# A hybrid decoder layer on one core: 192 columns of first weights instead of 256, the rotary tables behind the first norm, the attention norm by halves, the first keys and values among the input tiles

## The chip, the core and the metric

One core of a Trainium2 chip runs the whole layer as one program. TensorE (PE) does the matrix products and reads its operands from SBUF, the on-chip memory; its sums arise in PSUM. VectorE (DVE), ScalarE (ACT) and GpSimd (POOL) do the elementwise work, and the queue of SyncE (SP) issues the DMAs between HBM and SBUF. Every engine works off its own instruction list in order, and they wait for one another by semaphores. The metric is the device time of one execution in microseconds (us), the median over runs; lower is better.

## The reference

The layer has sequence length 1024, width 1024, 8 attention heads and float32 throughout. Shortened:

```
u = rmsnorm(h, g_mix);  z = u @ w_in          # x_rnn 512 | x_gate 512 | c_q 256 | c_kv 128 | k_rope 32
y_rnn = rglru_group(x_rnn, x_gate, ...)       # conv over 4 steps, two gates, linear recurrence, gelu(x_gate)
q  = rmsnorm(c_q) @ w_q_up                    # per head 64 nope + 32 rotary columns
kv = rmsnorm(c_kv) @ w_kv_up                  # per head 64 key + 64 value columns
q_rope, k_rope = apply_rope(...)              # cos and sin of position * frequency
y_att = causal softmax attention (8 heads, query blocks of 128)
h = h + concat(rmsnorm(y_rnn), rmsnorm(y_att)) @ w_out
h = h + (silu(rmsnorm(h) @ w_ffn_gate) * (rmsnorm(h) @ w_ffn_up)) @ w_ffn_down    # inner width 2816
h = h + sigmoid(rmsnorm(h) @ w_ple_gate) * rmsnorm(p @ w_ple_proj)
return rmsnorm(h, g_final)
```

## The kernel before

**Products.** Activations are kept transposed: features on the 128 partitions, the 1024 positions along the row. Each float32 operand is split into a high part and a low part of a shorter format, and each product is three matmuls, high by high, high by low and low by high (`x_h`, `x_l` and `w_h`, `w_l` in the trace). The usual matmul is 128x512: one 128x128 weight block against half of the positions.

**Order.** The code doesn't emit instructions as it goes. It records them in a `Plan`; `Plan.order` then runs a list scheduler with modelled costs over all engines, and on each engine takes the ready operation with the smallest key. The key is the number of the operation in the recording, plus `plan.shift` at that moment, plus a few fixed offsets (line 232). PSUM is given out in two pools, four banks of 512 columns and two wide buffers of 1024, and SBUF in 51 slots of one size; an operation can only start when its tile has a place. All instructions are emitted by one line (372), so every row of the trace has L372, and only names of tiles tell them apart.

**Stages, in the trace's time.**
- 0 to 39 us: the input `x` arrives in eight blocks k of 128 features (`xr`) and is split into `x_h` (ACT) and `x_l` (DVE); its squares are added up in `x_acc` (DVE). For each k the weights `w1[k]`, 256 columns wide, give two tiles `g`: `g1[0]` holds the 128 columns of c_kv, `g1[1]` the rotary key columns, k and its swapped halves, each laid out twice (32+32+32+32). Each block is 12 matmuls: 2 tiles, 2 halves of the positions, 3 products. In between stand the first products of c_q (`wn_a`, `wn_b`). `nx_ms` sums `x_acc` over the partitions, `nx_bc` spreads the reciprocal root over them, `nx_rb` is the copy of it with which every later tile is scaled (`ckv`, `krz`, `cq`, `zr`, `zg`).
- The generator `tables()` works out the angles (`ang`, `turns`), sine and cosine (`sc`, `cse`), and the constants of the recurrence (`q`, `cpos`).
- 50 to 165 us: eight input tiles in the order of `IN_ORDER` (`in_tile`, r0 to r3 recurrent, g0 to g3 gate), with the recurrence between (`rg_*`). Behind the last but one come the rotary keys (`make_rope_keys`), the keys of the first heads (`make_k`, tiles `kps`, `k_h`, `k_l`), queries (`make_q`, `qps`) and values (`make_v`, `v`).
- 165 to 350 us: attention head by head (`s` scores, `pA` and `pB` exponentials, `tp` transposes, `av`), with the first half of the output product (`wo<-yr`) in between. `ya` is the attention's result, four tiles of 1024 positions; `y_acc` the sum of its squares.
- 338 to 428 us: the attention norm (`na_ms`, `na_bc`, `na_rb`), the scaled and split `ya_h` and `ya_l`, and the output product `wo`.
- 428 to 1057 us: the feed-forward layer. Its gate and up products use weights `wg`, `wu`; the inner activations `hx` go to HBM and come back for the down product, which runs over c = 0 to 3 (inner blocks) and j (output blocks), j = 0 to 15 in all. Each j needs a pair of weight tiles `wd_r`, which `pump("d", j)` loads and splits; each c needs its `hx` tiles, seven groups, worked off one after the other at the first j of the c.
- 1057 us to the end: the gated embedding (`plg`, `ple`) and the last norm.

Of the kernel before, what the change touches and what calls it, by code (L numbers as in the profile page):

```python
# [8 lines left out]
F32R = mybir.dt.float32r  # L9
BF16 = mybir.dt.bfloat16  # L10
I32 = mybir.dt.int32
AF = mybir.ActivationFunctionType
ALU = mybir.AluOpType
# [3 lines left out]
P = 128  # L17
S = 1024
# [25 lines left out]
IN_ORDER = "r0 r1 r2 r3 g0 g1 g2 g3".split()  # L44
# [334 lines left out]
XLATE = 40  # L379
HOLD = 0.15  # L380
KLATE = 100
HL = 5
HAT = 3
NWIDE = 2
# [8 lines left out]
def hybrid_layer(ctx, tc, xT, pT, pos, vec, const, const2, w1, wn, wrg, wq, wkv, wo, wg, wu, *rest):  # L393
    plan = Plan(tc.nc)
# [9 lines left out]
    def slot(name, dt=F32):  # L404
        return plan.tile(big, [P, S], dt, name, "slot", NSLOT)
# [29 lines left out]
    def f(ap):  # L435
        return ap.bitcast(F32)
# [19 lines left out]
    def load_w(src, name, cols=S):  # L456
        raw = wslot(name + "_raw")
        Y.dma_start(out=raw[:, :cols], in_=src)
        hi = wslot(name + "_h", F32R)
        lo = wslot(name + "_l", F32R)  # L460
        A.activation(hi[:, :cols], raw[:, :cols], AF.Copy)
        V.tensor_sub(lo[:, :cols], raw[:, :cols], f(hi)[:, :cols])
        return hi, lo

    Q = [slice(0, HB), slice(HB, S)]
# [34 lines left out]
            yield  # L500


    order = [(("w1", k), w1[k], 256) for k in range(8)] + [(("wn", i), wn[i], S) for i in range(2)]
    order += [(("rg", 0), wrg, S)] + [(("wn", i), wn[i], S) for i in range(2, 10)]
    order += [(("wkv", 0), wkv, S), (("wq", 0), wq[0], S)]
    order += [(("wq", 1), wq[1], S)]
# [20 lines left out]
    def col(name, i=0):  # L527
        c = VEC[name] + i
        return vc[:, c:c + 1]
# [65 lines left out]
    def tables():  # L595

        pi = slot("pos_i", I32)
        Y.dma_start(out=pi, in_=pos.to_broadcast([P, S]))
        ang = slot("ang")
        V.tensor_copy(ang, pi)  # L600
        V.tensor_scalar_mul(ang, ang, INVF)
        kk = slot("turns")
        V.tensor_scalar(kk, ang, 0.15915494309189535, 12582912.0, op0=ALU.mult, op1=ALU.add)
        V.tensor_scalar_add(kk, kk, -12582912.0)
        for cpart in (6.0, 0.28125, 0.0019353071795864769):
            V.scalar_tensor_tensor(out=ang, in0=kk, scalar=-cpart, in1=ang, op0=ALU.mult, op1=ALU.add)
        V.scalar_tensor_tensor(out=kk, in0=ang, scalar=-1.0, in1=ang, op0=ALU.mult, op1=ALU.max)
        V.tensor_scalar(kk, kk, BETA, GAMMA, op0=ALU.mult, op1=ALU.add)
        V.scalar_tensor_tensor(out=ang, in0=ang, scalar=ALPHA, in1=kk, op0=ALU.mult, op1=ALU.add)
        sc = slot("sc")  # L610
        yield
        A.activation(sc, ang, AF.Sin)
        cse = slot("cse")
        G.memset(cse[0:64], ATT_SCALE)
        A.activation(cse[64:128], sc[64:128], AF.Copy, scale=ATT_SCALE)


        plan.hold = plan.ops[-1]
        lL = vc[:, VEC["lru_L"]:VEC["lru_L"] + 4]
        nl, al, e4, s4, z4, po = [small([P, 4], f"q4_{i}", bufs=1) for i in range(6)]  # L620
        V.tensor_scalar_mul(nl, lL, -1.0)
        V.tensor_max(al, lL, nl)
        A.activation(e4, al, AF.Exp, scale=-1.0)
        V.tensor_scalar_add(s4, e4, 2.0)
        V.reciprocal(s4, s4)
        V.tensor_mul(s4, s4, e4)
        V.tensor_mul(z4, s4, s4)
        V.memset(po, 1.0 / 19.0)
        for d in (17, 15, 13, 11, 9, 7, 5, 3, 1):
            V.tensor_mul(po, po, z4)  # L630
            V.tensor_scalar_add(po, po, 1.0 / d)
        V.tensor_mul(po, po, s4)
        V.tensor_scalar_max(nl, nl, 0.0)
        V.scalar_tensor_tensor(out=po, in0=po, scalar=2.0, in1=nl, op0=ALU.mult, op1=ALU.add)
        cpos = small([P, 4], "cpos", bufs=1)
        cneg = small([P, 4], "cneg", bufs=1)
        V.tensor_scalar_mul(cpos, po, LRU_C)
        V.tensor_scalar_mul(cneg, po, -LRU_C)
        plan.hold = None
        tabs.extend((sc, cse, cpos, cneg))  # L640


# [3 lines left out]
    for k in range(8):  # L646
        xr = slot("xr")
        if k == 0:
            if X0 == 1:
                Y.dma_start(out=vc, in_=vec)  # L650
            if X0 == 2:
                Y.dma_start(out=xr[:, HS[0]], in_=xT[k][:, HS[0]])
                Y.dma_start(out=vc, in_=vec)
            wh, wl = weight(("w1", k), 0)
            x2 = (slot("x_h", F32R), slot("x_l", F32R))
            for h in range(2):
                if not (X0 == 2 and h == 0):
                    Y.dma_start(out=xr[:, HS[h]], in_=xT[k][:, HS[h]])
                A.activation(x2[0][:, HS[h]], xr[:, HS[h]], AF.Copy, scale=col("g_mix", 0))
                V.scalar_tensor_tensor(out=x2[1][:, HS[h]], in0=xr[:, HS[h]], scalar=col("g_mix", 0),  # L660
                                       in1=f(x2[0])[:, HS[h]], op0=ALU.mult, op1=ALU.subtract)
        else:
            Y.dma_start(out=xr, in_=xT[k])
            wh, wl = weight(("w1", k))
            x2 = split(xr, col("g_mix", k), "x")
        if k == 1:
            Y.dma_start(out=cs, in_=const)
        if k == TK:
            tb = tables()
            next(tb)  # L670
        xs.append(x2)

        plan.shift = XLATE
        sq_acc(acc, xr, k == 0, V)
        plan.shift = 0
        for i in range(2):
            c = slice(i * P, (i + 1) * P)
            mm(g1[i][:2], wh[:, c], wl[:, c], x2, k == 0, k == 7)

    if TK == 8:  # L680
        tb = tables()
# [157 lines left out]
    tasks.append(cq_task())  # L839
    step()  # L840
    rgw = weight(("rg", 0), 1)
    for it in IN_ORDER[:-1]:
        if it == "g2":
            weight(("wkv", 0), 0)
            weight(("wq", 0), 0)
        in_tile(it)


    wqr = {}
    qs, ks, vt = {}, {}, []  # L850
# [129 lines left out]
    ys = []  # L980
# [20 lines left out]
    def two():  # L1001
        return both("wo", len(ops) % 3 < 2)

    kvh, kvl = weight(("wkv", 0), 1)
    wqr[0] = weight(("wq", 0), 1)
    make_rope_keys()
    make_k(0)
    make_q(0, 0)
    in_tile(IN_ORDER[-1])
    for b in range(3):  # L1010
        make_v(b)
    step()
    for qb in range(4):
        scores(0, qb)
        make_v(3 + qb)
    make_q(0, 1)
    make_v(7)

# [76 lines left out]
    res = []  # L1095
    hs, xf, hd = {}, {}, {}
    facc = slot("f_acc")
    for _ in rstd_steps(yacc[0], 512, "na", res):
        pass
    for j in range(4):  # L1100
        V.tensor_mul(ya[j], ya[j], res[0])
        ys.append(split(ya[j], col("g_att", j), "ya"))

    def make_x(va, vb, name):

# [159 lines left out]
    def down(c, m, xs, mid, after=None):  # L1265
        j = 4 * c + m

        def ahead(i):
            pump("d", j)
            if i >= 3:  # L1270
                pump("d", j + 1)
            mid(i)
            if c == 0 and i == HAT and m < 3:
                reload_h(m + 1)
# [166 lines left out]
def _layout(a):  # L1441
# [14 lines left out]
    k[:, C_ID:C_ID + P] = np.eye(P)  # L1456
    i = np.arange(P)
    k2 = np.zeros((P, 2 * P), np.float32)
    k2[:, :P] = (i[:, None] < 64) & (i[:, None] % 32 == i[None] % 32)
    k2[:, P:] = np.where(i[None] > i[:, None], NEG, 0.0)  # L1460
    o["const2"] = k2
    r = i % 64
# [8 lines left out]
    ckv = np.r_[1280:1408]  # L1471
    kr = np.r_[1408:1440]
    ksw = np.r_[1424:1440, 1408:1424]
    o["w1"] = c(w3[:, :, np.concatenate([ckv, kr, ksw, kr, ksw])])

    def ntile(w, cols):
        return w[:, cols].reshape(-1, P, len(cols)).transpose(1, 0, 2).reshape(P, -1)
# [56 lines left out]
```

## Time and profile before

| What | Value |
|---|---|
| Median of 3 runs | 1192.4 us (1192.07 to 1193.71) |
| The profiled execution | 1192.32 us, of which the trace's span is 1190.5 us |
| Mean granted TensorE clock | 0.995 of full speed |
| PE busy | 1161.9 us, 98% of the span |
| DVE, ACT, POOL busy | 983.7, 646.4, 234.9 us |

The span reaches from the first to the last instruction; 1.8 us of the execution lie around it. "Busy" counts a matmul until its modelled end, and matmuls overlap, so PE can be busy and slow at once.

### The profile page before, as it was taken

How to read it: one execution, taken by the hardware profiler on the slowest of the kernel's cores; microseconds unless marked ns; L12 is line 12 of the kernel's file. 1: busy time of each engine (PE TensorE's matmuls, PEld its weight loads, DVE VectorE, ACT ScalarE, POOL GpSimd, SP SyncE). 2: the span in 40 equal slices, each digit the busy share in tenths (PEclk: the TensorE clock that was granted, in tenths of full speed). 3: DMA queues.
4: the chain of work that ended last, by engine and by line, in shares of the span. 5: the costliest groups of instructions: out<-in, count | busy, mean ns of one | idle time of the engine just before them, and what ended most of it. 6: DMA issues, size and time to landing. Idle time of an engine off the chain costs nothing.

```text
span 1190.5 us, 15414 instructions
## 1 busy us (share of the span) xinstructions
PE 1161.9 (98%) x5608; PEld 964.9 (81%) x5608; DVE 983.7 (83%) x1482; ACT 646.4 (54%) x1085; POOL 234.9 (20%) x133
## 2 busy tenths in 40 slices
PE   8999999999999999999999999999999999999996
PEld 6788878888878878888888888888887887887896
DVE  7978788888978599889888888878997758785987
ACT  8447977877846265454444544444332214376565
POOL 0001240312102132333123321333000000244000
PEclk9999999999999999999999999999999999999998
DMA  9001100000305123344423544266968764032342
GB/s 343 19 18 36 36 1 1 2 1 1 134 26 195 72 107 124 124 177 184 170 102 129 195 160 157 106 250 223 358 243 280 261 243 160 36 124 89 108 175 72
DMA packets 47676, 155.91 MB, mean 131 GB/s; under 512 B 5360, under 2 KB 8688, under 8 KB 47600
## 3 DMA queue, kind: packets, MB, share of 16 engines
q1 hardware_dynamic: 47600, 154.93, 35.5%
q8 instruction: 44, 0.72, 0.2%
q14 instruction: 32, 0.26, 0.1%
HBM read 109.82 MB, written 45.09 MB: 130 GB/s over the span
## 4 chain that ended last, share of the span: by engine, by line
PE 83%; DVE 9%; ACT 4%; DMA 2%; issue 2%; SPq 0%; DVEq 0%; ACTq 0%
PE ff_z L372 29%; PE ff_y L372 14%; PE ff_x L372 7%; PE wo L372 5%; PE plg L372 4%; PE s L372 4%; PE wn L372 4%; PE av L372 2%; PE tp L372 2%; PE qps L372 1%; PE wn_b L372 1%; PE wn_a L372 1%; DVE h L372 1%; DMA wd_r<-in_wd 1%; PE wo_a L372 1%
## 5 line engine op out<-in xcount | busy, mean ns | idle before, releaser
L372 POOL TENSOR_TENSOR silu<-silu,nf_rb 128x512 f32<-128x512 f32 x77 | 123.8, 1632 | 278.1 <-DVE silu L372 257.8
L372 PE MATMUL ff_z<-hx,wd 128*128 128x512 f32 x528 | 128.6, 390 | 2.9 <-ACT wd L372 1.7
L372 PE MATMUL ff_z<-x,wg 128*128 128x512 f32 x528 | 128.0, 390 | 0.2 <-DVE x L372 0.2
L372 PE MATMUL ff_z<-x,wu 128*128 128x512 f32 x528 | 127.1, 389 | 0.0
L372 PEld LDWEIGHTS ff_z<-hx,wd 128*128 128x128 f32 x528 | 98.5, 188 | 25.1 <-ACT wd L372 2.1
L372 PEld LDWEIGHTS ff_z<-x,wg 128*128 128x128 f32 x528 | 98.9, 188 | 21.8 <-DVE x L372 0.9
L372 PEld LDWEIGHTS ff_z<-x,wu 128*128 128x128 f32 x528 | 99.0, 188 | 20.7 <-ACT ff_u L372 0.2
L372 ACT ACTIVATE hx<-silu 128x512 fp32r<-128x512 f32 x55 | 34.6, 629 | 71.3 <-DVE silu L372 42.1
L372 PE MATMUL ff_y<-hx,wd 128*128 128x512 f32 x264 | 65.3, 389 | 0.0
L372 PE MATMUL ff_y<-x,wg 128*128 128x512 f32 x264 | 64.3, 390 | 0.7 <-ACT x L372 0.7
L372 PE MATMUL ff_y<-x,wu 128*128 128x512 f32 x264 | 63.6, 389 | 0.0
L372 ACT ACTIVATE wd<-wd_r 128x256 fp32r<-128x256 f32 (+2 forms) x64 | 29.9, 491 | 60.2 <-DMA wd_r<-in_wd 21.4
L372 PE MATMUL plg<-hg_h,wpg_h 128*128 128x256 f32 (+1 forms) x192 | 61.7, 321 | 0.6 <-ACT wpg_h L372 0.3
L372 PE MATMUL plg<-hg_l,wpg_h 128*128 128x256 f32 (+1 forms) x192 | 61.1, 318 | 0.0
L372 PE MATMUL plg<-hg_h,wpg_l 128*128 128x256 f32 (+1 forms) x192 | 61.0, 319 | 0.0
L372 DVE TENSOR_TENSOR h<-ff_z,h 128x512 f32<-128x512 f32 x64 | 43.8, 686 | 20.6 <-PE ff_z L372 20.2
L372 POOL TENSOR_TENSOR p_acc<-p_acc,sq 128x1024 f32<-128x1024 f32 x7 | 18.2, 2595 | 214.0 <-ACT sq L372 214.0
L372 PEld LDWEIGHTS ff_y<-x,wg 128*128 128x128 f32 x264 | 49.4, 188 | 11.5 <-ACT x L372 1.1
L372 PEld LDWEIGHTS ff_y<-hx,wd 128*128 128x128 f32 x264 | 49.6, 188 | 10.4
L372 PEld LDWEIGHTS ff_y<-x,wu 128*128 128x128 f32 x264 | 49.6, 188 | 10.3
L372 ACT ACTIVATE wd<-wd_s 128x256 fp32r<-128x256 f32 (+2 forms) x48 | 23.5, 498 | 63.3 <-DVE wd_s L372 48.1
L372 ACT ACTIVATE silu<-silu 128x512 f32<-128x512 f32 x44 | 27.8, 632 | 53.4 <-POOL silu L372 52.9
(407 smaller groups left out, 3048.2 us busy)
## 6 DMA issues: line engine op xcount, KB each, us to landing
hx<-hx SPq DMA_DIRECT2D x140, 512.0 KB, 3.8
wg_r<-in_wg SPq DMA_DIRECT2D x22, 512.0 KB, 5.1
wu_r<-in_wu SPq DMA_DIRECT2D x22, 512.0 KB, 3.4
wpg_raw<-in_wpg SPq DMA_DIRECT2D x20, 512.0 KB, 3.5
wn_raw<-in_wn SPq DMA_DIRECT2D x10, 512.0 KB, 7.2
wo_raw<-in_wo SPq DMA_DIRECT2D x8, 512.0 KB, 4.5
h<-in_xT SPq DMA_DIRECT2D x8, 512.0 KB, 4.4
hd<-h SPq DMA_DIRECT2D x8, 512.0 KB, 3.2
```

The costliest lines, as they stand in the source:

```text
L372: getattr(self.engines[o.eng], o.fn)(*a, **k)
```

## The change

Five things, each in its own place of the code:

1. `load_w` makes the low part only for the first 128 columns of a 192-column weight tile in a tile of its own; the low part of the 64 columns left over is written beside their high part, into columns 192 to 255 of the `hi` tile. The weights `w1` come with 192 columns (c_kv, the rotary columns once). So one 128-column block holds 64 high and 64 low columns of the rotary keys, and `g1[1]` takes four matmuls for each k (x_h and x_l, two halves) instead of six; high and low land in different rows of the result, which the constant matrix `const2` then adds together.
2. In `tables()` a shift of 300 is put on the angle tables and on the recurrence's constants.
3. The attention norm, with its scaling and splitting, has a shift of -200, and the first of the four `ya` tiles is scaled and split by halves of the positions.
4. `make_rope_keys` is called at tile g1, `make_k(0)` at g2, and four of the eight `make_v` ahead of the last input tile.
5. In the down product `pump("d", j + 1)` is called from step i = 1 of a j and no longer from i = 3.

```diff
+NV0 = 4
+TL = 300
+NAE = -200
...
-        V.tensor_sub(lo[:, :cols], raw[:, :cols], f(hi)[:, :cols])
+        full = cols - cols % P
+        V.tensor_sub(lo[:, :full], raw[:, :full], f(hi)[:, :full])
+        if full < cols:
+            V.tensor_sub(hi[:, cols:full + P], raw[:, full:cols], f(hi)[:, full:cols])
...
-    order = [(("w1", k), w1[k], 256) for k in range(8)] + [(("wn", i), wn[i], S) for i in range(2)]
+    order = [(("w1", k), w1[k], 192) for k in range(8)] + [(("wn", i), wn[i], S) for i in range(2)]
...
+        plan.shift = TL
         V.tensor_copy(ang, pi)
...
+        mm(g1[0][:2], wh[:, :P], wl[:, :P], x2, k == 0, k == 7)
         for i in range(2):
-            c = slice(i * P, (i + 1) * P)
-            mm(g1[i][:2], wh[:, c], wl[:, c], x2, k == 0, k == 7)
+            for h in range(2):
+                T.matmul(g1[1][h], lhsT=wh[:, P:2 * P], rhs=x2[i][:, HS[h]], start=k == 0 and i == 0, stop=k == 7 and i == 1)
...
-    kvh, kvl = weight(("wkv", 0), 1)
+    for it in IN_ORDER[:-1]:
+        if it == "g1":
+            kvh, kvl = weight(("wkv", 0), 0)
+            make_rope_keys()
+        if it == "g2":
+            weight(("wq", 0), 0)
+            make_k(0)
+        in_tile(it)
+    for b in range(NV0):
+        make_v(b)
     wqr[0] = weight(("wq", 0), 1)
-    make_rope_keys()
-    make_k(0)
     make_q(0, 0)
     in_tile(IN_ORDER[-1])
-    for b in range(3):
-        make_v(b)
     step()
     for qb in range(4):
         scores(0, qb)
-        make_v(3 + qb)
+        if NV0 <= 3 + qb:
+            make_v(3 + qb)
...
+    plan.shift = NAE
     for _ in rstd_steps(yacc[0], 512, "na", res):
         pass
     for j in range(4):
-        V.tensor_mul(ya[j], ya[j], res[0])
-        ys.append(split(ya[j], col("g_att", j), "ya"))
+        hi, lo = slot("ya_h", F32R), slot("ya_l", F32R)
+        for c in HS if j == 0 else [slice(0, S)]:
+            V.tensor_mul(ya[j][:, c], ya[j][:, c], res[0][:, c])
+            A.activation(hi[:, c], ya[j][:, c], AF.Copy, scale=col("g_att", j))
+            V.scalar_tensor_tensor(out=lo[:, c], in0=ya[j][:, c], scalar=col("g_att", j), in1=f(hi)[:, c],
+                                   op0=ALU.mult, op1=ALU.subtract)
+        ys.append((hi, lo))
+    plan.shift = 0
...
             pump("d", j)
-            if i >= 3:
+            if i >= 1:
                 pump("d", j + 1)
...
-    k2[:, :P] = (i[:, None] < 64) & (i[:, None] % 32 == i[None] % 32)
+    k2[:, :P] = i[:, None] % 32 == i[None] % 32
...
-    o["w1"] = c(w3[:, :, np.concatenate([ckv, kr, ksw, kr, ksw])])
+    o["w1"] = c(w3[:, :, np.concatenate([ckv, kr, ksw])])
```

**The first place is DVE between the last blocks of `x` and the first norm.** Before, the angle table's instructions stand between the sums of squares:

```order
L372 SCALAR_TENSOR_TENSOR x_l<-xr,vc,x_h 128x1024
L372 SCALAR_TENSOR_TENSOR ang<-turns,ang 128x1024
L372 TENSOR_TENSOR x_acc<-x_acc,sq 128x1024
L372 SCALAR_TENSOR_TENSOR ang<-turns,ang 128x1024
L372 TENSOR_TENSOR rg_l<-rg_raw,rg_h 128x1024
L372 SCALAR_TENSOR_TENSOR turns<-ang 128x1024
L372 TENSOR_TENSOR x_acc<-x_acc,sq 128x1024
L372 TENSOR_SCALAR turns<-turns,cs 128x1024
L372 TENSOR_TENSOR x_acc<-x_acc,sq 128x1024
L372 SCALAR_TENSOR_TENSOR ang<-ang,cs,turns 128x1024
```

Now the first of them stand behind the norm's last small operation (`n_r`), and ahead of the scaling of the first tiles:

```order
L372 TENSOR_TENSOR n_r<-n_r_403,n_t 128x8
L372 CAST ang<-pos_i 128x1024
L372 TENSOR_SCALAR ang<-ang,cs 128x1024
L372 TENSOR_SCALAR turns<-ang 128x1024
L372 TENSOR_TENSOR cq_438<-wn_a,nx_rb 128x512
L372 TENSOR_TENSOR ckv<-g_93,nx_rb 128x1024
L372 TENSOR_TENSOR krz<-g_100,nx_rb 128x1024
L372 TENSOR_TENSOR cq_438<-wn_b,nx_rb 128x512
L372 TENSOR_SCALAR turns<-turns 128x1024
L372 TENSOR_TENSOR wn_l<-wn_raw,wn_h 128x1024
L372 SCALAR_TENSOR_TENSOR ang<-turns,ang 128x1024 x3
```

All ten instructions on `ang` and `turns` have left the stretch ahead of `n_ss`, and three of them now precede the scaling that empties the PSUM tiles `g`.

**The second place is PE at the attention norm.** Names ending in `_h` and `_l` are high and low parts; what stands in brackets are the engines that a matmul waits for. Before, the first product of the new operand takes whole tiles:

```order
L372 MATMUL na_bc<-cs,n_r 128x128 [waits PE_49]
L372 MATMUL na_bc<-cs,n_r 128x128 x3
L372 MATMUL wo_b<-yr_l,wo_h 128x512
L372 MATMUL wo_a<-yr_h,wo_l 128x512
L372 MATMUL wo_b<-yr_h,wo_l 128x512
L372 MATMUL wo<-ya_h,wo_h 128x512 [waits Activation_49]
L372 MATMUL wo<-ya_h,wo_h 128x512 x3
L372 MATMUL wo_a<-ya_h,wo_h 128x512
L372 MATMUL wo_b<-ya_h,wo_h 128x512
L372 MATMUL wo<-ya_l,wo_h 128x512 [waits DVE_49]
```

Now:

```order
L372 MATMUL na_bc<-cs,n_r 128x128 x3
L372 MATMUL wo_a<-yr_h,wo_l 128x512
L372 MATMUL wo_b<-yr_h,wo_l 128x512
L372 MATMUL wo_a<-yr_h,wo_h 128x512
L372 MATMUL wo_b<-yr_h,wo_h 128x512
L372 MATMUL wo_a<-yr_l,wo_h 128x512
L372 MATMUL wo_b<-yr_l,wo_h 128x512
L372 MATMUL wo_a<-yr_h,wo_l 128x512
L372 MATMUL wo_b<-yr_h,wo_l 128x512
L372 MATMUL wo<-ya_h,wo_h 128x512 [waits Activation_49]
L372 MATMUL wo<-ya_h,wo_h 128x512
L372 MATMUL wo_a<-ya_h,wo_h 128x512
```

Eight old products now stand behind `na_bc` where there were three, and the wait for the second half of `ya_h` comes three matmuls later.

**The third place is SP's queue in the down product**, around the weights of j = 12, the first j of c = 3. Before:

```order
L372 DMA hx<-hx_5_6247 128x1024
L372 DMA hx<-hx_5_6553 128x1024
L372 DMA hx<-hx_5_6859 128x1024
L372 DMA wd_r_8567<-in_wd 128x1024
L372 DMA wd_r_8577<-in_wd 128x1024
L372 DMA hx<-hx_5_7208 128x1024
```

Now:

```order
L372 DMA hx<-hx_4_7166 128x1024
L372 DMA wd_r_8541<-in_wd 128x1024
L372 DMA wd_r_8551<-in_wd 128x1024
L372 DMA hx<-hx_5_6242 128x1024
L372 DMA hx<-hx_5_6548 128x1024
L372 DMA hx<-hx_5_6854 128x1024
L372 DMA hx<-hx_5_7203 128x1024
```

The pair of `wd_r` has moved ahead of three tiles of the sixth `hx` group; at j = 8 it has moved ahead of two in the same way.

## Rows read from the trace of the kernel before

**Rows 1.** What PE waited for over the whole span: total, times, longest.
```profile
PE wo L372 <- ACT ya_h L372: 2.5, 1, 2.5
PE ff_z L372 <- ACT wd L372: 1.7, 1, 1.7
PE v L372 <- DVE v L372: 1.6, 1, 1.6
PE s L372 <- ACT pB L372: 1.4, 2, 1.2
PE ff_z L372 <- DVE h L372: 1.2, 1, 1.2
PE wn_a L372 <- DVE wn_l L372: 0.6, 1, 0.6
```

**Rows 2.** The chain that ended last: start us, us, what, in the down product.
```profile
973.32 9.31 DMA wd_r<-in_wd
...
1016.41 2.72 PE ff_x L372 x12
```

**Rows 3.** Timeline of PE in the first stage: start us, us, operation, tiles, count.
```profile
14.29 0.73 PE L372 MATMUL g<-x_l,w_h 128*128 128x512 f32 x2
...
39.24 0.99 PE L372 MATMUL nx_ms<-cs,x_acc 128*128 128x128 f32 x7
```

**Rows 4.** Timeline of DVE in the first stage.
```profile
12.96 1.28 DVE L372 SCALAR_TENSOR_TENSOR x_l<-xr,vc,x_h 128x1024 fp32r<-128x1024 f32 x1
...
37.96 1.22 DVE L372 TENSOR_TENSOR x_acc<-x_acc,sq 128x1024 f32<-128x1024 f32 x1
```

**Rows 5.** Windows, instructions on the tile ang alone: window, length, DVE busy (count), ACT busy, clock.
```profile
20.00:41.00 21.00, 8.29 (x8) 0.59 (x1) 1.00 0.44 177
```

**Rows 6.** Timeline of ACT at the end of the first norm.
```profile
48.34 0.60 ACT L372 ACTIVATE nx_rb<-nx_bc 128x512 f32<-128x512 f32 x1 [0.52 <-PE nx_bc L372]
```

**Rows 7.** Timeline of DVE before the attention.
```profile
114.42 2.28 DVE L372 TENSOR_TENSOR_SCAN rg_h<-rg_r,rg_i 128x1024 f32<-128x1024 f32 x1
...
148.12 3.90 DVE L372 TENSOR_TENSOR_SCAN rg_h<-rg_r,rg_i 128x1024 f32<-128x1024 f32 x1
152.03 3.73 DVE L372 TENSOR_TENSOR k_l<-kr,k_h 64x512 fp32r<-64x512 f32 x6
...
164.41 4.26 DVE L372 TENSOR_TENSOR v<-v 128x256 fp32r<-128x256 f32 x12
```

**Rows 8.** Timeline of POOL in the same stretch.
```profile
147.02 2.85 POOL L372 TENSOR_TENSOR r_acc<-r_acc,sq 128x1024 f32<-128x1024 f32 x1 [13.52 <-ACT sq L372]
```

**Rows 9.** Windows of the input tiles: PE, PEld, DVE, ACT, POOL busy (counts), clock, DMA share, GB/s.
```profile
50.00:160.00 110.00, 110.00 (x503) 91.33 (x502) 92.31 (x112) 73.40 (x83) 16.44 (x6) 1.00 0.07 25
```

**Rows 10.** Timeline of ACT at the first scores.
```profile
174.79 0.69 ACT L372 ACTIVATE pA<-s,nm 128x512 f32<-128x512 f32 x1 [0.29 <-DVE nm L372]
```

**Rows 11.** Timeline at the attention norm, of PE, ACT and DVE.
```profile
346.25 1.03 PE L372 MATMUL na_bc<-cs,n_r 128*128 128x128 f32 x8
...
346.94 1.09 ACT L372 ACTIVATE na_rb<-na_bc 128x512 f32<-128x512 f32 x2 [3.48 <-PE na_bc L372]
...
348.06 3.50 DVE L372 TENSOR_TENSOR ya<-ya,na_rb 128x1024 f32<-128x1024 f32 x3 [3.55 <-ACT na_rb L372]
...
349.32 3.48 ACT L372 ACTIVATE ya_h<-ya,vc 128x1024 fp32r<-128x1024 f32 x3 [1.29 <-DVE ya L372]
...
350.52 1.20 PE L372 MATMUL wo<-ya_h,wo_h 128*128 128x512 f32 x4 [2.55 <-ACT ya_h L372]
```

**Rows 12.** Windows at the attention norm and in the down product, columns as in rows 9.
```profile
350.00:355.00 5.00, 4.23 (x11) 2.96 (x12) 5.00 (x5) 2.76 (x3) 0.00 (x0) 0.66 0.00 0
...
980.00:985.00 5.00, 3.32 (x15) 2.31 (x14) 2.72 (x5) 2.02 (x4) 0.00 (x0) 1.00 1.02 419
```

**Rows 13.** Timeline of PE in the down product, at j = 8.
```profile
915.92 0.39 PE L372 MATMUL ff_x<-hx,wd 128*128 128x512 f32 x1
917.54 1.67 PE L372 MATMUL ff_z<-hx,wd 128*128 128x512 f32 x6 [1.23 <-DVE h L372]
```

More of the change, by code (lines that the diff above doesn't have):

```diff
@@ L610, in tables @@
         sc = slot("sc")
+        plan.shift = 0
         yield
+        plan.shift = TL
         A.activation(sc, ang, AF.Sin)
@@ L639, in tables @@
         plan.hold = None
+        plan.shift = 0
         tabs.extend((sc, cse, cpos, cneg))
@@ L841, in hybrid_layer @@
     rgw = weight(("rg", 0), 1)
[L842 to L846, printed above, removed]
     wqr = {}
@@ L1100, in hybrid_layer @@
     for j in range(4):
-        V.tensor_mul(ya[j], ya[j], res[0])
-        ys.append(split(ya[j], col("g_att", j), "ya"))
+        hi, lo = slot("ya_h", F32R), slot("ya_l", F32R)
[5 more added lines that the diff above has]
+        ys.append((hi, lo))
+    plan.shift = 0
     def make_x(va, vb, name):
```

## The prediction

> **What bounds the kernel now.** I read first what PE waited for. Six of the waits of over half a microsecond lie in stretches that the change reorders [rows 1]; the longest others, for the first input and in the last norm, lie outside them. Then the chain that ended last: it is nearly all PE, and twelve 128x512 matmuls take 2.72 us of it, so 0.227 us is the price of one at full clock [rows 2]. So the time is the number of matmuls times 0.227 us, plus the waits, plus what a low clock adds; DVE matters only where PE waits for it. One correction goes with every wait: a matmul is shown with 0.39 us [rows 13] but the next may start after 0.227 us, so a wait costs 0.16 us more than its idle time says.
>
> **Part 1, the narrow weights, with the tables behind the norm (part 2).** Eight blocks k lose 2 matmuls each: 16 x 0.227 = 3.6 us. Not all of it is on the path. The low part of x for k = 2 sets a matmul at 14.29 [rows 3], since DVE works on it from 12.96 for 1.28 us [rows 4], and DVE's work ahead of it stays: a 256-column low part becomes one of 128 and one of 64. The four matmuls that k = 0 and 1 lose only lengthen the wait there (0.9 us lost), and at k = 3 the next low part, a DVE round later, takes another 0.4. From 14.29 on, the new order has 80 matmuls until `nx_ms` (of 104, 24 stand ahead), so PE gets there at 14.29 + 80 x 0.227 + 0.4 = 32.8. Before it was 39.24 [rows 3] with 33 more matmuls; 16 of them are gone and 17 come later, worth 17 x 0.227 = 3.9 us. The gain is 39.24 - 3.9 - 32.8 = 2.5 us.
>
> It stands only if `x_acc` is ready by then. Before, it was ready at about 39.1 [rows 4], with the table work in front: eight instructions on `ang` with 8.3 us [rows 5], two on `turns` alone of about 0.7 each, and one of those on `ang` (1.28) after `x_acc`, so some 8 us. In the new order DVE has from 12.96 on six low parts at 1.2, six sums at 1.13, four low parts of weights of the same form and three narrow pairs at 0.33 (neighbours overlap by 0.08): 19.5 us, done at 32.5. That is 0.3 us ahead of PE, the narrowest place in this sum. Bounds: with `x_acc` two instructions later, 2.3 us, the gain is about nothing; with no loss at the starts it is 3.6.
>
> The wait for `wn_l`, 0.6 us [rows 1], goes with the table work ahead of it: 0.7 us gained (bounds 0 and 0.7). What is late next: the first matmul behind `nx_bc` now waits for the bank that ACT's copy `nx_rb` empties. The copy starts 0.52 after it could go on and takes 0.60 [rows 6], while PE has its second half of `nx_bc` to do: about 0.35. And `ckv`, which empties a `g` tile for the next wide product, is queued on DVE behind three table instructions of about 0.6 each, which start when `n_r` is done: about 0.3 late. So 2.5 + 0.7 - 0.65, and 0.15 off for the narrow place: **2.4 us** (0 to 4.3).
>
> **Part 4, keys and values among the input tiles.** Before the attention PE waits 1.6 us for `v` and 1.4 for two exponentials: 3.0 us [rows 1]. On DVE a scan of 3.90 us, six low parts of rotary keys with 3.73 and twelve pieces of v with 4.26 stand in a row there [rows 7], and PE consumes what comes of them at once. Afterwards the keys, and v for four blocks, lie under tiles whose matmuls need nothing of them. One exponential still has to come back before the next scores have a bank: 0.69 us for 512 columns [rows 10]; with its start after the row's maximum and two such places I put 0.7 back. **2.3 us** (0 to 3.0). The cover that hides the moved work is the input tiles: from 50 to 160 PE is never idle and DVE is busy for 92.3 of 110 us [rows 9]. The keys are inside that window before and after; the table's 9.7 us come in anew: 102 of 110.
>
> Here a rule bears on it. The scan that begins at 148.12 takes 3.90 us, another one 2.28 [rows 7], and POOL's addition runs from 147.02 for 2.85 [rows 8]: the 1.6 us too many are the 1.75 us of POOL's that were left. The Trainium skill, "GPSIMD Engine Reference", section Specifications, says that POOL's SBUF interfaces are shared with VectorE and contend with DVE instructions that have two SBUF inputs or a two-port mode. These rows agree. By the rule the moved instructions would meet POOL's as well, which is the last rival below.
>
> **Part 3, the norm by halves.** Before, PE ran out of old products and idled 2.55 us until ACT had `ya_h` [rows 11], 2.7 with the correction. Then it ran at the low of its two levels for a while: the granted clock from 350 to 355 is 0.66 of full speed, a mean of its two levels, 1.2 and 2.4 GHz, and 11 matmuls begin there [rows 12], where the 4.5 us left would hold 19.8: 2.0 us lost (0.25 of it a second wait). Together 4.7. By halves the chain is: `na_bc` to `na_rb` 0.69 us, `na_rb` half of 1.09, `ya` half of 1.17, `ya_h` half of 1.16, each with its handover, about 2.7 us instead of 4.27 [rows 11]. From its start on PE now has 0.9 us of `na_bc` itself and 8 old products, 1.8: 2.7. So the long wait closes to about nothing, and what remains is the first half of `ya_l`, which stands behind a whole `ya` on DVE (1.17): about 0.4, and a rest of 0.2. The window with the wait of 1.7 us in the down product has a clock of 1.00 [rows 12], the one after 2.55 us has not; so a wait under half a microsecond should keep it. **4.1 us** (2.5, if the clock falls all the same, to 4.7). The stall doesn't move on to the feed-forward layer: what starts there hangs on the last `wo` products, which move up with it.
>
> **Part 5, the down weights.** At j = 8 PE waits 1.23 us and at j = 12 1.7 [rows 1, 13], 3.2 with the corrections. At j = 12 the weight is issued at 973.32 and lands 9.31 us later [rows 2]; the DMA engines run at 1.02 of their share, 419 GB/s [rows 12]. Three `hx` tiles of 512 KB issued ahead of it take 3.7 us at that rate. With the weight ahead of them it lands at about 979, splitting takes 0.7 us, and PE wants it at 981.5. The `hx` tiles come 2.5 us later for it, but theirs is the sixth of seven groups of 2.72 us, first needed 13.6 us after the first one. At j = 8 it is the same with two tiles. **3.2 us** (1.4, if only j = 8 pays, to 3.3).
>
> **Sum.** 2.4 + 2.3 + 4.1 + 3.2 = 12.0 us. The profiled execution took 1192.3, with 1.8 us of it outside the span; 1192.3 - 12.0 = 1180.3, and as the median of the runs lies 0.1 higher, **1180.4 us**.
>
> **Rivals.**
> - *The start is DVE's.* `x_acc` is late, or PE at 5 to 14 us starts and stops and rises to full clock later. For it: only 0.3 us of margin. Against: 8 us of DVE work have gone. Part 1 gives 0: 1182.8.
> - *The attention's wait moves.* v and keys come in time, but the scores then wait for exponentials that ACT cannot make faster. For it: half of the 3.0 us is already that wait [rows 1]. Part 4 gives 0: 1182.7.
> - *The weight lands no earlier.* Its issue waits for a free slot, or the queue is what is full [rows 12]. Then j = 12 keeps its 1.8 us: 1182.2; with j = 8 as well the change does nothing there: 1183.6.
> - *DVE's backlog in the input tiles, the slower side.* 102 of 110 us leaves 8 free; if all of POOL's 16.4 us [rows 9] met DVE anew, PE would wait 16.4 - 8 = 8.4 us for scaled tiles: 1188.8. Taken in waits of 2.55 us, each would cost 2.0 more of low clock, as at 350 [rows 11, 12]: 8.4 x (1 + 2.0 / 2.55) = 15, and 1195.4, slower. It reaches the old time when the backlog is 12.0 / 1.78 = 6.7 us. Against: POOL's 16.4 us already lie beside a busy DVE, so most of it is in the 92.3.
>
> **How the numbers follow.** The forecast with all four parts has 0.58, its own range 1177.5 to 1182 from the bounds that go upwards and half a microsecond to each downwards. The start 0.14, the attention 0.12, the weights 0.08; two of these together, inside their shares, give about 1185 to 1186. The backlog 0.08, of which 0.04 ends slower and 0.02 about level. The range of 8 in 10 is 1177.5 to 1186.5. About 0.2%, 2.4 us, is what a measurement of this kernel can tell from no change; faster than 1190.0 has 0.93, within 0.03, slower 0.04.
>
> **What would show it.** In the trace after: `nx_ms` at 32.8 with an idle time under 0.3; no wait for `wn_l`, one of about 0.35 for `nx_rb`; PE without idle time from there to the attention, and there no wait for `v`; at the attention norm idle times under half a microsecond and a granted clock of 1.00; no wait for `wd` and `h` at j = 8 and 12. I am wrong if PE shows idle times between 50 and 160, if waits of over 1 us stand ahead of the first `s`, or if the low clock appears in the first 30 us or at the norm.

## The result and the profile after

The changed kernel takes 1181.4 us (median of 5 runs, 1180.33 to 1182.18) and the kernel before, beside it, 1193.7 us (5 runs, 1192.07 to 1194.92): a ratio of 0.9899, 95% interval 0.9885 to 0.9914: 1.0% faster, with the whole interval below 1. The profiled execution took 1181.38 us with a span of 1179.6; before it was 1190.5, so 10.9 us are to be found. By the medians it is 12.3 us, because the traced execution of the kernel before (1192.3) lies on the short side of its runs: beside the experiments they took 1190.5 to 1194.6 us where the mean granted clock was 0.995 to 0.997, and 1193.6 to 1197.1 where it was 0.993 or 0.994; none of the latter was traced. The stages are read from the starts of the same matmuls in both traces:

| Stage, from PE start to PE start | before | after | gained | foretold |
|---|---|---|---|---|
| Parts 1 and 2: start to the norm of c_kv (`nk_bc`) | 78.12 | 75.37 | 2.75 | 2.4 |
| Part 4: on to the recurrent norm (`nr_bc`) | 146.45 | 144.11 | 2.34 | 2.3 |
| Part 3: on to the first feed-forward product | 198.75 | 194.57 | 4.18 | 4.1 |
| to the first product on `hx` | 423.00 | 422.98 | 0.02 | 0 |
| Part 5: first to last product on `hx` | 213.22 | 211.58 | 1.64 | 3.2 |

Three terms of the sum hold within 0.4 us. One, the down weights, is half of what was foretold.

What PE waited for in the changed kernel over the span (total, times, longest); the rows that answer to [rows 1]:

```profile
PE g L372 <- DVE x_l L372: 1.0, 2, 0.7
PE ff_z L372 <- DVE h L372: 1.0, 1, 1.0
...
PE wn_b L372 <- DVE k_l L372: 0.4, 1, 0.4
PE s L372 <- ACT pB L372: 0.4, 1, 0.4
...
PE wn_a L372 <- ACT nx_rb L372: 0.3, 1, 0.3
```

`ya_h`, `v`, `wn_l` and ACT's `wd` are gone from the list; the sum `h` at j = 8 is still there, 1.0 instead of 1.2 us. A wait is named here after the j whose weights DVE splits meanwhile. PE itself is not there yet: by the count of matmuls it waits 48 of them ahead of its first product of j = 8, and in the kernel before 29.

Timeline of PE in the first stage and at the attention norm of the changed kernel, which answer to [rows 3] and [rows 11]:

```profile
14.39 0.73 PE L372 MATMUL g<-x_l,w_h 128*128 128x512 f32 x2 [0.67 <-DVE x_l L372]
...
33.09 1.03 PE L372 MATMUL nx_ms<-cs,x_acc 128*128 128x128 f32 x8
...
40.79 0.50 PE L372 MATMUL wn_a<-x_h,wn_h 128*128 128x512 f32 x1 [0.31 <-ACT nx_rb L372]
...
340.02 1.03 PE L372 MATMUL na_bc<-cs,n_r 128*128 128x128 f32 x8
...
342.85 0.73 PE L372 MATMUL wo<-ya_h,wo_h 128*128 128x512 f32 x2
```

`nx_ms` starts at 33.09 without a wait (foretold 32.8), where before it started at 39.24. The products on `ya_h` start 2.83 us after `na_bc`, without a wait; before it was 4.27 with 2.55 us of idle time.

Windows of the changed kernel, columns as in [rows 9] (the first row of [rows 12], the stretch behind the wait for `ya_h`, answers to the first two):

```profile
340.00:345.00 5.00, 5.00 (x25) 3.54 (x23) 3.65 (x5) 3.58 (x5) 0.00 (x0) 1.00 0.00 0
345.00:350.00 5.00, 5.00 (x23) 4.17 (x23) 4.97 (x6) 2.31 (x2) 0.00 (x0) 1.00 0.00 0
50.00:160.00 110.00, 109.57 (x500) 90.91 (x499) 94.12 (x129) 75.32 (x88) 18.72 (x7) 1.00 0.07 25
```

The granted clock stays at the upper level behind the norm (1.00, before 0.66). Among the input tiles PE loses 0.43 us in all, to one wait for a low part of the keys, and DVE is busy for 94.1 us, not the 102 of the prediction.

Down product of the changed kernel at j = 8, the chain that ended last (start us, us, what):

```profile
896.93 0.34 DVE wd L372
...
897.29 4.85 DMA wd_r<-in_wd
...
902.23 0.53 ACT wd L372
...
902.79 0.56 DVE wd L372
903.35 0.61 DVE h L372
...
904.00 3.06 PE ff_z L372 x12
```

The transfer is issued when a piece of DVE's splitting frees a place, and takes 4.85 us; ACT and DVE split the first piece; only then does DVE add up a sum `h`, and only then has PE a bank. PE wants the weight itself only at 915.09, 13 us after it landed. At j = 12 the weight is issued at 962.86 and lands at 970.01, ACT's first split starts at 970.10, PE's first product of that j at 972.45, and PE has no wait over 0.1 us there.

### The profile page after: what moved, and what is told of

It is laid out like the page before. It is cut to its first block, busy times and chain, and to the rows that moved or that the text cites. A ratio compares the mean times of both kernels' runs of the same rounds, so it can differ in the third digit from the quotient of the medians.

```text
span 1179.6 us, 15387 instructions
## 1 busy us (share of the span) xinstructions
PE 1156.2 (98%) x5592; PEld 960.3 (81%) x5592; DVE 977.4 (83%) x1492; ACT 643.8 (55%) x1084; POOL 237.9 (20%) x133
## 4 chain that ended last, share of the span: by engine, by line
PE 88%; DVE 6%; ACT 4%; issue 1%; DMA 1%; SPq 0%; DVEq 0%; ACTq 0%
PE ff_z L372 30%; PE ff_y L372 15%; PE ff_x L372 7%; PE wo L372 5%; PE plg L372 4%; PE s L372 4%; PE wn L372 4%; PE av L372 2%; PE tp L372 2%; PE wn_b L372 2%; PE wn_a L372 2%; PE qps L372 1%; DVE h L372 1%; PE wo_b L372 1%; PE wo_a L372 1%
## 5 line engine op out<-in xcount | busy, mean ns | idle before, releaser
L372 DVE TENSOR_REDUCE nm<-s 128x1 f32<-128x128 f32 (+3 forms) x64 | 48.1, 751 | 10.2 <-PE s L372 9.6
```

The source lines that it names most:

```text
L372: getattr(self.engines[o.eng], o.fn)(*a, **k)
```

## The experiments

All are edits of the changed kernel and compute the whole layer. Each ratio is to the kernel before on the same chip; the first four kernels, the next four and the last three each shared a chip. Most intervals overlap with that of the changed kernel, so a difference of 1 to 2 us is read from the stage. The changed kernel and late6 were profiled twice, and their stretch on `hx` came out the same within 0.04 us. That is not the whole spread: where every engine has the changed kernel's order, the stretch on `hx` took 210.15 to 211.61 us (seven executions of six kernels), and the first stage 74.84 to 75.90 us (ten executions). What makes most of both is said below.

| Kernel | median us | ratio, 95% interval | stage it was made for: us, against the changed kernel |
|---|---|---|---|
| pump3 | 1181.5 | 0.9916, 0.9903 to 0.9930 | `hx`: 213.89, +2.3 |
| early_dma | 1182.0 | 0.9913, 0.9899 to 0.9926 | `hx`: 212.67, +1.1 |
| whole | 1183.3 | 0.9930, 0.9917 to 0.9944 | norm: 196.59, +2.0 |
| nae0 | 1182.9 | 0.9925, 0.9911 to 0.9938 | norm: 195.74, +1.2 |
| tl0 | 1185.7 | 0.9934, 0.9918 to 0.9951 | first: 80.22, +4.9 |
| w256 | 1184.2 | 0.9925, 0.9907 to 0.9943 | first: 78.92, +3.6 |
| keys_late | 1183.0 | 0.9914, 0.9895 to 0.9933 | attention: 146.39, +2.3 |
| late6 | 1179.8 | 0.9884, 0.9868 to 0.9901 | `hx`: 210.33, -1.3 |
| changed again | 1182.4 | 0.9899, 0.9882 to 0.9916 | `hx`: 211.61, 0 |
| late6 again | 1179.4 | 0.9879, 0.9861 to 0.9897 | `hx`: 210.32, -1.3 |
| late8 | 1182.0 | 0.9899, 0.9881 to 0.9918 | `hx`: 212.51, +0.9 |

**Part 5 undone.**

```diff
-            if i >= 1:
+            if i >= 3:
                 pump("d", j + 1)
```

> The changed kernel with part 5 undone (the next down weights pumped from i = 3 again). Theory, from the trace after: part 5 took away the wait at j = 12 (1.84 us from start to start, less the spacing) and only 0.2 of the one at j = 8, and gave 0.2 back in small waits; so this kernel is 1.65 us slower than the changed one, about 1183.0 us, with a wait of about 1.2 us for DVE's h in front of j = 8 and one of about 1.7 for wd at j = 12. The prediction's own account: both waits had gone, 3.2 us slower, 1184.6. Rival, part 5 is worth nothing and the gain at the end of the down product came from elsewhere: 1181.4.

Measured: 2.3 us more in the stretch on `hx`, so between the two figures. The waits are not simply those of before: 0.5 for `h`, 0.8 and 1.1 for `wd`. Yet every engine has the order of the kernel before in this stretch, where it took 213.22: the same order meets other landing times. Against the seven executions with the changed order (210.15 to 211.61) the part is worth 1.6 to 3.7 us.

**The issue earlier, the split where it was.** Each call of `pump` takes one step of loading and splitting; now there is one call at i = 1 and the next only at i = 4.

```diff
-            if i >= 1:
+            if i == 1 or i >= 4:
                 pump("d", j + 1)
```

> The changed kernel with the weights' DMA issued as early as there (one pump at i = 1), but their splitting put back to where it stood before (pumps from i = 4). Theory: at j = 8 PE waits because DVE works in order and the first split of the new weights, which needs the landing, stands ahead of the sums h that empty PE's banks; the change moved the split up by as much as the landing. Here the split is behind the landing, so the wait of 1.0 us ahead of j = 8 goes and none comes back at j = 12: 1.2 us faster than the changed kernel, 1180.2 us. Rival, the landing itself is what PE waits for at j = 8: the same as the changed kernel, 1181.4. Second rival, the split now comes too late for its own products: waits for wd at the start of some j, 0.5 to 2 us slower, 1182 to 1183.4.

Measured: 1.1 us more. The wait for `h` at j = 8 is gone, as the theory has it, but two others have come, at j = 9 and at j = 12. PE and DVE of this kernel at j = 9:

```profile
918.93 2.32 PE L372 MATMUL ff_z<-hx,wd 128*128 128x512 f32 x9 [1.41 <-ACT wd L372]
```

```profile
914.74 0.56 DVE L372 TENSOR_TENSOR wd<-wd_r,wd 128x384 fp32r<-128x384 f32 x1 [1.84 <-ACT wd L372]
915.66 0.56 DVE L372 TENSOR_TENSOR wd_s<-wd_r,wd_r 128x384 f32<-128x384 f32 x1 [0.37 <-DMA wd_r<-in_wd]
916.14 0.69 DVE L372 TENSOR_TENSOR h<-ff_z,h 128x512 f32<-128x512 f32 x1
...
918.14 0.69 DVE L372 TENSOR_TENSOR h<-ff_z,h 128x512 f32<-128x512 f32 x1
```

The row of PE names ACT, and a split of ACT ends at the same 918.83 as the sum of 918.14. But ACT and DVE had made all seven splits for j = 8 by 912.3; what they split here is for j = 9, and by the count PE is still at the third of seven products of j = 8, which goes into the bank that this sum empties. DVE idled 1.84 and 0.37 us ahead of pieces whose weights were not there, with sums behind them. So it is one kind of wait in three places: **a sum that frees a PSUM bank stands on DVE's in-order list behind a split that waits for a transfer.** None of the three expectations gave that the wait would reappear at other j.

**The planner told that a weight lands later.** The planner decides the order on DVE by the time at which it believes a transfer lands: 2.1 us plus the bytes at 360 GB/s, 3.2 us for these 393 KB. The trace shows 4.85 us at j = 8, and 9.31 for the 512 KB of j = 12 before [rows 2]. The Trainium skill, "DMA: Bandwidth & Descriptors", section "Anatomy of one DMA — SWDGE (gpsimd) path", has nearly the planner's rule, about 2.0 us plus the bytes at 436 GB/s, for a path of issue that is not the one here; an estimate by it is 2.9 us. The row differs, and the row decides.

```diff
-            return v.shape[0] * v.width() * 4 / 360e3, 2.1
+            return v.shape[0] * v.width() * 4 / 360e3, 6.0 if v.buf.name.startswith("wd_r") else 2.1
```

> The changed kernel with one number of the planner's model altered: it believes that the down weights land 6.0 us plus their size after their issue instead of 2.1 (in the trace they take 4.9 to 9). SP's order around j = 8 and j = 12 stays, but on DVE the first split of j = 8's weights now stands behind five sums h more. Theory, DVE's in-order queue holds back the sums that empty PE's banks whenever a split waits for a landing: the wait of 1.0 us ahead of j = 8 goes and none comes at j = 9 to 12, 1.2 us or a little more faster than the changed kernel, 1180.0 us, 209.9 to 210.4 us from the first to the last matmul on hx (211.6 in the changed kernel). Rival, the landing itself is what the weights' products wait for: no change, 1181.4. Second rival, the splits are now too late for their own products: a wait for wd at j = 8 of 1 us or more, 1182 or over.

Measured: 1.25 us less and no wait ahead of j = 8, as the theory had it; a wait of 0.48 us for `wd` at j = 12 it had not. The order of SP is the same, and the weight of j = 8 lands no earlier (issued at 898.56, there at 902.42; in the changed kernel 897.29 and 902.15; in both the first product on `hx` starts at 837.03). DVE of this kernel there:

```profile
901.25 0.69 DVE L372 TENSOR_TENSOR h<-ff_z,h 128x512 f32<-128x512 f32 x1 [0.67 <-PE ff_z L372]
902.61 0.69 DVE L372 TENSOR_TENSOR h<-ff_x,h 128x512 f32<-128x512 f32 x1 [0.67 <-PE ff_x L372]
903.97 0.69 DVE L372 TENSOR_TENSOR h<-ff_z,h 128x512 f32<-128x512 f32 x1 [0.67 <-PE ff_z L372]
905.33 0.69 DVE L372 TENSOR_TENSOR h<-ff_z,h 128x512 f32<-128x512 f32 x1 [0.67 <-PE ff_z L372]
905.94 0.55 DVE L372 TENSOR_TENSOR wd<-wd_r,wd 128x384 fp32r<-128x384 f32 x1
```

Every sum follows its product (the releaser is PE each time), and the split comes without a wait behind them. Whether this is a better kernel was then measured beside the changed one:

> The changed kernel as it is, on the same chip as the two kernels below, so that they can be compared with it directly. Expected: a ratio to the kernel before near 0.990, as at the first measurement, and the wait of about 1.0 us for a sum h at j = 8 again.

> The kernel whose planner believes that a down weight lands 6.0 us after its issue, once more, beside the changed kernel on the same chip. If the 1.25 us that its trace showed in the stretch on hx are a property of the order, its median is about 1.3 us under that of the changed kernel and the wait at j = 8 is absent again; if the difference was one of two executions, the medians agree within 0.5 us.

Measured: 1182.4 us (1180.18 to 1182.63) and 1179.4 (1179.20 to 1180.22). The stretch is 1.29 us shorter again, and the wait at j = 8 absent. The rest of the 3.0 us is not shown to be the edit's: 0.98 us of it is the start of the first norm (33.53 against 32.55), with transfers of the input that land up to 1 us earlier in the one execution. So against the changed kernel the edit gains 1.3 us in its stretch, and by the median this is the fastest version.

Three kernels that have the old belief and an edit elsewhere (whole, w256, keys_late) also came to 210.15 to 210.55. Their edits have not moved the order: on every engine it is that of the changed kernel in this stretch. What differs is how long the first weight of j = 8 takes from issue to landing, and the wait goes with it:

| Changed order, execution | landing of the weight, us | PE's wait for `h` at j = 8, us | stretch on `hx`, us |
|---|---|---|---|
| changed | 4.85 | 1.00 | 211.58 |
| nae0 | 4.76 | 0.90 | 211.54 |
| changed again | 4.73 | 0.88 | 211.61 |
| whole | 4.56 | 0.70 | 210.53 |
| tl0 | 4.34 | 0.48 | 211.25 |
| w256 | 4.21 | 0.36 | 210.55 |
| keys_late | 3.81 | under 0.1 | 210.15 |

Within 0.02 us the wait is the landing less 3.85 in every row that has one, as it should be if DVE's list stands still for the transfer; smaller waits elsewhere make the rest of the last column. (In the order of before it is the landing less 3.78: 1.23 us for 5.01, and 0.48 for 4.27 in pump3.) Why the same weight lands in 3.8 us in one execution and in 4.8 in another is not shown. So the belief of 6.0 takes away the dependence on this landing; where the landing is quick, the order of the old belief does as well.

> The belief is 8.0 us instead of 6.0. Theory (PE pays when the split of a weight and a sum stand in the wrong order on DVE, either way round): no gain beyond that of 6.0; where landing takes 5 us, as at j = 8, the split now stands behind sums that it doesn't need, so waits of PE for wd of 0.5 us or more appear, and the stretch on hx takes 210.5 to 212 us. Rival (later is always safer, since only the sums are held up): the 0.5 us that are left at j = 12 with the belief of 6.0 go as well, and the stretch takes 209.6 to 210.0 us.

Measured: 212.51, no gain. The 0.5 us at j = 12 stay (`wd`, 0.48), so the rival falls. The stretch is 2.2 us longer than with 6.0 and above the theory's range. The largest new loss, about half of it, is another than the theory named: it is not for `wd`. PE, DVE and POOL of this kernel at the last j:

```profile
1036.21 3.00 PE L372 MATMUL ff_z<-hx,wd 128*128 128x512 f32 x12 [0.89 <-DVE h L372]
```

```profile
1031.93 3.54 DVE L372 SCALAR_TENSOR_TENSOR hg_l<-h,vc,hg_h 128x1024 fp32r<-128x1024 f32 x1 [1.31 <-POOL p_acc L372]
1035.39 0.68 DVE L372 TENSOR_TENSOR h<-ff_z,h 128x512 f32<-128x512 f32 x1
1035.99 1.27 DVE L372 SCALAR_TENSOR_TENSOR hg_l<-h,vc,hg_h 128x1024 fp32r<-128x1024 f32 x1
```

```profile
1029.49 4.89 POOL L372 TENSOR_TENSOR p_acc<-p_acc,sq 128x1024 f32<-128x1024 f32 x2 [14.22 <-ACT sq L372]
```

A sum again stands behind something that is late, here a low part for the next stage, 3.54 us long where its neighbour takes 1.27. At j = 12 the first split stands behind a sum that it does not need. The belief of 6.0 can't be told to be the best, only better than 2.1 and 8.0 in the executions here.

**The norm: halves and shift, one at a time.**

```diff
-        for c in HS if j == 0 else [slice(0, S)]:
+        for c in [slice(0, S)]:
```

> The changed kernel with the first tile of the attention norm scaled and split whole again, the shift of -200 kept. Theory: from na_bc to ya_h take 4.27 us as before, PE has 0.9 us of na_bc and eight products (1.8) to do, so it idles about 1.4 us ahead of wo<-ya_h and 0.25 ahead of ya_l, and at that length the granted clock stays at 1.00: 1.8 us slower than the changed kernel, 1183.2 us. Rival, any long wait there brings the low clock as it did before the change (0.66 in the window from the first of the new products on): 2 us more, 1185.2.

```diff
-NAE = -200
+NAE = 0
```

> The changed kernel with halves, but no shift for the attention norm: na_bc has only three old products behind it. Theory: the chain by halves takes 2.7 us, cover is 0.9 and 0.7: an idle time of about 1.1 us, clock 1.00, 1.2 us slower than the changed kernel, 1182.6. Rival, the halves alone do it and the shift is worth nothing: 1181.4. Second rival, the clock falls: 1184.6.

Measured: 2.0 and 1.2 us more. Without the halves, PE of that kernel and the windows behind:

```profile
343.71 1.20 PE L372 MATMUL wo<-ya_h,wo_h 128*128 128x512 f32 x4 [1.40 <-ACT ya_h L372]
...
346.00 0.73 PE L372 MATMUL wo<-ya_l,wo_h 128*128 128x512 f32 x2 [0.63 <-DVE ya_l L372]
```

```profile
345.00:350.00 5.00, 4.37 (x20) 3.31 (x19) 4.47 (x4) 1.49 (x2) 0.00 (x0) 1.00 0.00 0
350.00:355.00 5.00, 5.00 (x24) 4.12 (x23) 2.51 (x2) 0.96 (x2) 0.00 (x0) 1.00 0.00 0
```

The two waits are there, and the clock is 1.00 behind them: it cost nothing more. The rival with the low clock falls. In the kernel without the shift it is one wait of 1.1 us, again at a clock of 1.00. So what one of them gives alone is its wait, and the 2.0 us that the low clock took before [rows 11, 12] come back as soon as either stands, in one execution of each.

**The first stage: narrow weights alone, tables behind the norm alone.**

```diff
-TL = 300
+TL = 0
```

> The changed kernel with the tables' shift at 0 again: the ten instructions on ang and turns stand in front of the first norm, the weights stay narrow. Theory: DVE then ends x_acc at about 40.5, PE has done its 130 matmuls by 39.0 and waits for nx_ms, and once more for nx_bc; the narrow weights give nothing back alone, so this kernel is 2.5 to 3 us slower than the changed one, 1184.2 us. Rival, the matmuls that are left out count alone: the same as the changed kernel, 1181.4.

```diff
-    order = [(("w1", k), w1[k], 192) for k in range(8)] + ...
+    order = [(("w1", k), w1[k], 256) for k in range(8)] + ...
...
-    o["w1"] = c(w3[:, :, np.concatenate([ckv, kr, ksw])])
+    o["w1"] = c(w3[:, :, np.concatenate([ckv, kr, ksw, kr, ksw])])
```

(with the products and `const2` of before).

> The changed kernel with 256 columns of first weights and twelve matmuls for each block again, the tables behind the norm. Theory: PE has 16 matmuls more before nx_ms, of which 4 fall into the wait for x_l of k = 2 and some of one more: 2.4 us slower than the changed kernel, 1183.8. Rival, all 16 count: 3.6 us, 1185.0. Second rival, DVE sets the end of the stage anyway (x_acc is 0.3 us ahead of PE): the same, 1181.4.

Measured: 4.9 us more with the narrow weights alone. About 1.0 of it is not the edit's: DVE's list stands still until the constants `cs` have landed, ahead of the low part of x for k = 1, and they come later in this execution. DVE of the changed kernel and of this one:

```profile
9.20 0.23 DVE L372 CAST ib<-cs 128x128 bf16<-128x128 f32 x1 [2.17 <-DMA cs<-in_const]
```

```profile
10.18 0.23 DVE L372 CAST ib<-cs 128x128 bf16<-128x128 f32 x1 [2.73 <-DMA cs<-in_const]
```

The other 3.9 us make the stage 1.1 longer than in the kernel before, where that cast starts at 9.15. (The spread of the first stage goes with the same landing: in the ten executions with the changed order it ends 66.1 to 66.3 us after the cast starts, which is at 8.57 to 9.75.) With the tables moved alone it is 3.6 more, of which 0.9 is a late landing of the second half of the first block of `x`; the rest is near the 2.4 expected, and the stage is as long as before. There the last `x_acc` ends at 33.97 and PE comes to `nx_ms` at 36.69 without a wait: the count of matmuls sets the end. PE and DVE of the kernel with the narrow weights alone:

```profile
41.48 0.66 PE L372 MATMUL nx_ms<-cs,x_acc 128*128 128x128 f32 x4 [0.67 <-DVE x_acc L372]
...
48.98 0.62 PE L372 MATMUL nx_bc<-cs,n_r 128*128 128x128 f32 x4 [0.59 <-DVE q L372]
...
50.29 0.65 PE L372 MATMUL nx_bc<-cs,n_r 128*128 128x128 f32 x4 [0.69 <-ACT nx_rb L372]
```

```profile
39.01 1.28 DVE L372 SCALAR_TENSOR_TENSOR ang<-ang,cs,turns 128x1024 f32<-128x1024 f32 x1
40.21 1.21 DVE L372 TENSOR_TENSOR x_acc<-x_acc,sq 128x1024 f32<-128x1024 f32 x1
41.34 1.22 DVE L372 TENSOR_TENSOR wn_l<-wn_raw,wn_h 128x1024 fp32r<-128x1024 f32 x1
```

Fewer matmuls don't help where DVE sets the end: `x_acc` ends at 41.4, behind the table's `ang`, and PE waits for it. That is the first rival, which did not come true in the changed kernel, brought about by taking away one half of it.

**Keys and values late, as before.**

```diff
-        if it == "g1":
-            kvh, kvl = weight(("wkv", 0), 0)
-            make_rope_keys()
...
-            make_k(0)
         in_tile(it)
-    for b in range(NV0):
-        make_v(b)
...
+    make_rope_keys()
+    make_k(0)
     make_q(0, 0)
     in_tile(IN_ORDER[-1])
+    for b in range(3):
+        make_v(b)
```

> The changed kernel with part 4 undone: rotary keys, keys and values behind the last but one input tile again. Theory: the waits for v and for the exponentials come back, 2.3 us slower than the changed kernel, 1183.7, with no wait of 0.4 for k_l at 134 us. Rival, the waits had gone for another reason (DVE was relieved by what else moved): the same, 1181.4.

Measured: 2.3 us more in the stage it was made for, no wait for `k_l` among the input tiles, and these waits of PE are back:

```profile
PE v L372 <- DVE v L372: 1.6, 1, 1.6
PE s L372 <- ACT pB L372: 1.4, 2, 1.2
```

## Why the prediction was right, and where not

- **Parts 1 and 2: right, 2.75 us for 2.4.** The count of matmuls from 14.39 on and the margin held: the last `x_acc` ends at 32.7, 0.4 us ahead of PE (foretold 0.3). The wait for `nx_rb` is 0.31 (0.35). That the size came within 0.35 us is in part luck: with the same order the stage varies by 1.06 us with the landing of `cs`, which the prediction did not look at. It had said that the narrow weights gain only if the tables' work is out of the way; that moving the tables gains nothing without the narrow weights it had not said, and the two experiments show both.
- **Part 4: right, 2.34 us for 2.3**, and by the experiment it is this part's. One wait of 0.4 us for `k_l` came anew among the input tiles.
- **Part 3: right, 4.18 us for 4.1.** That a short wait does not bring the low clock was an assumption from one window; waits of 1.40, 0.63 and 1.1 us at a clock of 1.00 bear it out.
- **Part 5: mis-sized, 1.64 us for 3.2.** The step that failed is "At j = 8 it is the same with two tiles". At j = 12 it was right: PE waited for the weight itself, and the weight now lands 2.4 us before PE wants it (foretold 2.5). At j = 8 the row named a sum `h`, and I priced it as if it were the weight; but the weight had landed at 914.02, 10 us before PE's first product of j = 8 (924.37). The issue moved up by two products, and so did the split on DVE, and with it the place where a sum is held up: the wait stays what the landing takes less 3.8 us, in the old order as in the new, and 1.23 us became 1.00 only because 5.01 became 4.85. Small new waits took back about 0.6. The experiment with the belief of 6.0 us, which moves the split, issues the weight 1.3 us later and lands it no earlier, takes the wait away. [rows 1] had said it: one wait names `wd`, the other `h`. The size alone would not show the fault, since 3.2 lies within the 1.6 to 3.7 that the two orders differ by from execution to execution.
- **The backlog in the input tiles** did not come: the 102 us of DVE assumed that all of the table's work falls between 50 and 160. Windows on `ang` alone in the changed kernel (window, length, DVE busy, clock, DMA share, GB/s):

```profile
38.00:50.00 12.00, 6.06 (x7) 1.00 0.10 38
50.00:160.00 110.00, 2.25 (x2) 1.00 0.07 25
```

  Three quarters of the work on `ang` are done by 50, before that window.
- The sum was 12.0 us and the span fell by 10.9: 1.6 too much in part 5, and 0.5 too little in the other four stages. With the time outside the span unchanged at 1.8 us, that is the whole difference between 1180.4 and 1181.4. Both count from the traced execution of 1192.3 us; had the prediction counted from the 1193.7 measured beside the changed kernel, its 12.0 would have ended at 1181.7, near the 1181.4 although part 5 was mis-sized.

## What to carry to other kernels

Where PE waits for a sum that empties a bank, look on the engine that makes the sum for what stands ahead of it: an instruction that waits for a transfer holds up everything behind it, and bringing the transfer forward brings its user forward too. A list scheduler places that instruction by the landing time that it believes; take that time from the trace under load, and expect it to differ from one execution to the next. And two edits that shorten the same stretch on two engines have to be costed together: fewer matmuls and less DVE work gave nothing here one by one.

## What was not expected of the hardware

DVE and POOL hold each other up in either order. The scan that took 3.90 us [rows 7] beside POOL's addition takes 2.28 in the changed kernel, and the addition near it is the slow one now. DVE and POOL of the changed kernel:

```profile
146.63 2.28 DVE L372 TENSOR_TENSOR_SCAN rg_h<-rg_r,rg_i 128x1024 f32<-128x1024 f32 x1
148.83 1.20 DVE L372 TENSOR_TENSOR wq_l<-wq_raw,wq_h 128x1024 fp32r<-128x1024 f32 x1
```

```profile
148.45 3.85 POOL L372 TENSOR_TENSOR r_acc<-r_acc,sq 128x1024 f32<-128x1024 f32 x1 [17.72 <-ACT sq L372]
158.89 2.42 POOL L372 TENSOR_TENSOR r_acc<-r_acc,sq 128x1024 f32<-128x1024 f32 x1 [6.60 <-ACT sq L372]
```

POOL came while DVE was at work, and took 1.43 us longer than the same addition ten microseconds later; DVE lost nothing. In the run with the belief of 8.0 us it was the other way round: the second of POOL's two additions (4.89 us for both) ends at about 1034.4, and 3.54 us of `hg_l` from 1031.93 are what was left of it, 2.45, and about the 1.27 of its neighbour, 3.7. The Trainium skill, "SBUF — State Buffer", section "SBUF: two separate sides", says that a DVE instruction with two SBUF inputs and a GpSimd one that reads SBUF take a shared pair of ports as an exclusive lock, whoever starts first, and the other blocks. Both cases agree with that rule within 0.2 us: POOL's 3.85 us are the 1.58 until DVE ended `wq_l` at 150.03, and 2.42 of its own, 4.0. In neither was the one that came first slowed, as it would be if the two shared the bandwidth.
